# A two-layer trunk on one core: the step into the second layer, and V in natural order

## Chip, cores and metric

The kernel runs on one core of a Trainium2 chip. The metric is the device time of one execution in microseconds; lower is better. Operands and results are 32-bit floats.

## What is computed

The reference is a trunk of two layers over 512 latent tokens and 256 context tokens, each a row of 1024. Every layer has a mixer (two attentions A and B and a gated MLP, fed by one projection `w_in` of the normalised and modulated input) and a mixture of 16 experts in which each expert chooses its tokens: 64 latent and 32 context tokens.

```python
h  = modulate(rmsnorm(x,  g_norm1[i]), sh1,  sc1)
hc = modulate(rmsnorm(xc, g_norm1[i]), sh1c, sc1c)
ka, va, kb, vb, qa, qb, u, v, gates = _split(h @ w_in[i], ...)
...
x = x + gt1 * branch_merge(ya, yb, yc, gates, w_branch[i], w_out[i])
...
x  = x  + gt2  * ec_moe(h2,  w_router[i], w_e1[i], w_e3[i], w_e2[i])
if not last:
    xc = xc + gt2c * ec_moe(h2c, w_router[i], w_e1[i], w_e3[i], w_e2[i])
...
def ec_moe(h, w_r, w1, w3, w2):
    aff = softmax(h @ w_r)
    gate, idx = lax.top_k(swapaxes(aff, 1, 2), cap)
    xin = h[idx]
    hid = silu(xin @ w1) * (xin @ w3)
    ye  = (hid @ w2) * gate
    return zeros.at[idx].add(ye)
```

The last step of a layer, `zeros.at[idx].add(ye)`, is a sum by token index: a token that several experts chose gets the sum of their rows. The output is the latent stream after a final norm.

## The kernel before

**Stages.** A mixer over the context alone (`c0`), one over the latent tokens (`c1`), routing, the experts of layer one (`experts_quad(0)`, L1259), the step into layer two, the mixer of layer two (`c2`, latent tokens, with keys and values of the context), routing, and the experts of layer two (`experts_tiled(1)`), with the final norm. `run()` (L1543) calls them in this order. Instructions of an engine run in the order in which they stand in its queue; a scheduling layer below the program moves them, and the sections on the change show where they stand.

**Weights in two parts.** A product that needs a split weight takes three PE products: high by high, high by low, low by high (`PAIRS`). `split_w` makes the parts: a rounding copy on ACT (L153) and a subtraction on DVE (L155), each 128x1024. They lie in six "w" buffers, so three split chunks fit. The raw chunks come in on SP's queue (`load_w`, L147).

**Experts of layer one.** 96 rows (64 latent, 32 context) are gathered for an expert (L1289, POOL's queue). `mm_set` (L1271) lays the work out in four groups of 32 columns of the array: a 256-wide quarter of the model dimension in each. `stage_1` and `stage_3` make silu and product (L1340), `stage_h` transposes the result (L1321, copies L1325), `stage_2` multiplies by w_e2, scales with the gate (L1347) and adds the rows into the residual in DRAM, in three scatters per expert on POOL's queue (L1349); each scatter waits for the landing of the one before. The loop runs one expert ahead: iteration e makes w_e1 of e+1, then w_e2 of e and w_e3 of e+1. PE's matmul records count two per instruction here.

**The last expert.** Its w_e2 goes another way (`stage_2_rows`, L1353): split weights, 48 products of 128x96 by 512 (L1281), one row scatter, and the rows kept in SBUF. `stage_x` (L1366) loads a table of token numbers (iota, L1369), compares it with the expert's indices to a 96x768 one-hot (L1373), and loads the six residual tiles of 128 tokens from DRAM (L1377), which therefore hold the scatters up to expert 14. `settle(i)` (L1380) adds expert 15's rows to tile i: one-hot by rows on PE (L1386, two halves of 512, two products each), and an add on DVE (L1388).

**The step.** `run()` loads four chunks of the next `w_in` early, settles and normalises tiles 0 to 3 (latent), then 4 and 5 (context), then transposes and modulates (`g_hT`: transposes L301, modulation L307 on ACT, high part L308, low part L309 on DVE) and starts the first keys and queries (`g_qk`, products L327). `norm_tile` (L284) is a square with a sum on ACT (L288), a small scale on DVE (L165), a power on POOL (L167) and a scaling on DVE (L289), in place.

**V.** `g_values` (L368) makes V per chunk of 128 columns in transposed form (weight chunk stationary, tokens moving, L327), copies it to SBUF (L391), transposes it on PE (L380) and copies the 128x128 blocks into V (L382). It runs for both attentions in `c0`, `c1` and `c2`: six passes, 96 transposes.

Memory for tiles is shared by tags; a tile waits until the one that had its buffer is done with. PSUM has four tiles of one bank ("p1") and two of two banks ("p2").

## Time and profile before

| | |
|---|---|
| three runs | 2655.39, 2658.69, 2649.29 us (median 2655.39) |
| the profiled execution | 2656.01 us |
| its span in the profile | 2654.2 us |
| PE busy | 2475.0 us (93%) |
| DVE, ACT, POOL busy | 1318.8, 813.9, 163.4 us |
| bytes moved by DMA | 646.49 MB, mean 244 GB/s |
| mean granted clock of PE | 0.974 |

The profile shows one execution. "Busy" is the time in which an engine ran an instruction; PE's matmul ends are modelled. A row of the timeline gives start, length, engine, line, operation, output and input by the program's names, and the count; in brackets stands the idle time of the engine just before and what ended it. The granted clock is TensorE's, as a share of full speed. SPq and POOLq are the queues in which an engine issues DMAs.

### The profile page before, as it was taken

The numbers are of one execution on the slowest core, as the hardware profiler recorded it, in microseconds if no ns is written. First come the engines' busy times: TensorE is split into PE (matmuls) and PEld (weight loads), VectorE is DVE, ScalarE is ACT, GpSimd is POOL, SyncE is SP. The second block draws the span as 40 slices with busy tenths as digits, with TensorE's granted clock in tenths as the row PEclk, the third lists the DMA queues.
The fourth block names the chain that finished last, engine by engine and source line by source line (L and its number), as shares of the span: only waits on it lengthen the run. The fifth ranks groups of instructions, "written<-read, shape, count | busy, mean of one in ns | idle before, by whom it ended". The sixth has DMA issues, their size and how long they took to land. (4 is left out here: it accounts for less than half of the span.)

```text
span 2654.2 us, 47903 instructions
## 1 busy us (share of the span) xinstructions
PE 2475.0 (93%) x19838; PEld 1709.1 (64%) x19838; DVE 1318.8 (50%) x2608; ACT 813.9 (31%) x1745; POOL 163.4 (6%) x169
## 2 busy tenths in 40 slices
PE   7999999999999979999999699999899969999997
PEld 5888877777778746666666487888788843332222
DVE  7767776878696431111111555656764352332223
ACT  4556455445533300000000445534453220000001
POOL 0000000001000011111111100000000010000000
PEclk9999999999999989999999899999999979999999
DMA  7674664353246779999999553252223569999997
GB/s 277 193 245 151 210 205 133 116 154 102 65 152 229 257 285 379 391 389 383 382 384 395 164 171 120 76 165 74 70 80 125 205 242 413 415 413 414 414 414 292
DMA packets 190954, 646.49 MB, mean 244 GB/s; under 512 B 22352, under 2 KB 32592, under 8 KB 190736
## 3 DMA queue, kind: packets, MB, share of 16 engines
q1 hardware_dynamic: 174352, 608.23, 62.6%
q0 software_dynamic: 10960, 21.50, 3.2%
q10 hardware_dynamic: 5424, 13.70, 1.8%
q8 instruction: 156, 2.56, 0.4%
q14 instruction: 62, 0.51, 0.1%
HBM read 612.94 MB, written 19.92 MB: 238 GB/s over the span
## 5 line engine op out<-in xcount | busy, mean ns | idle before, releaser
L327 PE MATMUL p<-h,w 128*128 128x512 f32 (+1 forms) x4416 | 913.9, 357 | 13.8 <-DVE w L155 5.8
L327 PEld LDWEIGHTS p<-h,w 128*128 128x128 f32 x4416 | 706.3, 190 | 133.9 <-DVE w L155 8.0
L155 DVE TENSOR_TENSOR w<-raw,w 128x1024 fp32r<-128x1024 f32 x224 | 273.5, 1222 | 226.5 <-ACT w L153 223.2
L153 ACT CAST w<-raw 128x1024 fp32r<-128x1024 f32 x224 | 235.1, 1050 | 372.1 <-PE p L327 138.7
L1271 PE MATMUL p<-h,k 128*32 128x256 f32 x3744 | 205.7, 379 | 0.0
L467 PE MATMUL p<-y,w 128*128 128x512 f32 (+1 forms) x864 | 176.6, 361 | 1.1 <-DVE w L155 1.1
L1271 PEld LDWEIGHTS p<-h,k 128*32 128x32 f32 x3744 | 121.2, 110 | 80.1 <-issue 1.2
L264 DVE SCALAR_TENSOR_TENSOR w<-raw,raw 128x1024 bf16<-128x1024 f32 x128 | 155.8, 1221 | 27.6 <-DMA raw<-in_w_adaT 21.4
L467 PEld LDWEIGHTS p<-y,w 128*128 128x128 f32 x864 | 144.3, 191 | 28.0 <-DVE w L155 1.5
L167 POOL TENSOR_TENSOR st<-st,mhalf 128x1 f32<-128x1 f32 x76 | 55.2, 726 | 1619.7 <-DVE st L165 1340.0
L1334 ACT ACTIVATE v<-p 128x768 f32<-128x768 f32 x16 | 13.0, 811 | 458.3 <-PE p L1271 458.3
L1434 PE MATMUL p<-h,k 128*64 128x512 f32 x528 | 128.3, 604 | 8.0 <-DMA h<-in_w_e 7.8
L492 PE MATMUL p<-k,q 128*128 128x256 f32 (+1 forms) x576 | 108.8, 319 | 29.0 <-DMA q<-q 20.0
L1509 DVE TENSOR_TENSOR y<-y,p 128x512 f32<-128x512 f32 x128 | 82.5, 684 | 81.7 <-PE p L1505 81.3
L492 PEld LDWEIGHTS p<-k,q 128*128 128x128 f32 x576 | 84.8, 194 | 44.5 <-issue 11.3
L1349 POOL DMA_INDIRECT x1a<-tg,idx x45 | 69.7, 1549 | 425.3 <-DVE tg L1347 216.1
L1095 PE MATMUL p<-w,h 128*128 128x512 f32 x384 | 91.3, 395 | 1.6 <-DVE w L155 1.1
L1347 DVE SCALAR_TENSOR_TENSOR tg<-p,gate,q 128x256 f32<-128x256 f32 x45 | 19.0, 478 | 142.7 <-PE p L1271 142.7
L1340 DVE TENSOR_TENSOR v<-v,p 128x768 f32<-128x768 f32 x16 | 15.3, 954 | 146.2 <-PE p L1271 137.1
L1434 PEld LDWEIGHTS p<-h,k 128*64 128x64 f32 x528 | 32.9, 136 | 85.3 <-issue 53.4
L1271 PE MATMUL p<-raw,k 128*32 128x256 f32 x1560 | 87.2, 379 | 0.5 <-ACT k L1328 0.5
L1306 DVE TENSOR_TENSOR k<-p,modAlat 128x256 f32<-128x256 f32 x32 | 13.4, 420 | 149.1 <-ACT k L1328 105.0
(339 smaller groups left out, 3128.2 us busy)
## 6 DMA issues: line engine op xcount, KB each, us to landing
h<-in_w_e SPq DMA_DIRECT2D x288, 512.0 KB, 10.7
raw<-in_w_in SPq DMA_DIRECT2D x164, 512.0 KB, 3.8
raw<-in_w_e SPq DMA_DIRECT2D x120, 512.0 KB, 10.1
e<-in_w_e SPq DMA_DIRECT2D x97, 512.0 KB, 10.4
m<-in_w_e SPq DMA_DIRECT2D x94, 512.0 KB, 10.6
raw<-in_w_adaT SPq DMA_DIRECT2D x80, 512.0 KB, 4.5
w<-in_w_e SPq DMA_DIRECT2D x66, 512.0 KB, 10.2
y<-in_w_e SPq DMA_DIRECT2D x52, 512.0 KB, 10.7
```

What stands on the lines that cost most here:

```text
L153: nc.scalar.copy(hi, fr(raw))
L155: nc.vector.tensor_sub(lo, fr(raw), fr(hi))
L167: nc.gpsimd.tensor_tensor(out=r, in0=v, in1=self.mhalf, op=ALU.pow)
L264: nc.vector.scalar_tensor_tensor(out=dump, in0=fr(raw), scalar=1.0, in1=self.cb[v], op0=ALU.mult, op1=ALU.mult, accum_out=self.mod[s, l][: ...
L327: nc.tensor.matmul(ps, lhsT=w[a][:, k * P:(k + 1) * P], rhs=h[k][:, b, :], start=(k == 0 and i == 0), stop=(k == KD - 1 and i == 2))
L467: nc.tensor.matmul(bps, lhsT=wb[a][:, (jj * 4 + k) * P:(jj * 4 + k + 1) * P], rhs=y[k][:, b, :], start=(k == 0 and i == 0), stop=(k == 3 a ...
L492: nc.tensor.matmul(ps, lhsT=Q[:, h, i, qs], rhs=k, start=(i == 0), stop=(i == 1))
L1095: nc.tensor.matmul(banks[i][hf], lhsT=c.mh[k][:, a, i * P:(i + 1) * P], rhs=w[b][:, hf * BW:(hf + 1) * BW], start=(k == 0 and p == 0), sto ...
L1271: nc.tensor.matmul(ps[32 * q:32 * q + 32, r * QW:(r + 1) * QW], lhsT=xT[:, k, 32 * r:32 * r + 32], rhs=w[:, q * QW:(q + 1) * QW], start=(k ...
L1349: nc.gpsimd.indirect_dma_start(out=dst4, out_offset=bass.IndirectOffsetOnAxis(ap=self.idx4[:, r, e:e + 1], axis=0), in_=y[:, r, :], in_off ...
L1434: nc.tensor.matmul(ps[half(h), :], lhsT=xT[:, k, :], rhs=w[:, h * BW:(h + 1) * BW], start=(k == 0), stop=(k == KD - 1))
L1509: nc.vector.tensor_add(xs[i][:, hs], xs[i][:, hs], pss[h])
```

## The change

Six parts, with the names of the new file where they differ:

1. The last expert's w_e2 goes the way of the others, in `last_ctx` (the 32 context rows: 32 products, one column group of 256 wide each per k and quarter) and `last_lat` (the 64 latent rows: 64 products), both over one set of eight raw chunks.
2. Experts 14 and 15 are not scattered. Their scaled rows stay in SBUF as (quarter, row) by 256 columns, and `settle` adds both: for each quarter q the products use the 32 array rows of group q, 8 products for a context tile, 16 for a latent one, each 128x256 into its own PSUM bank. The one-hots are made in `stage_hot`, one expert earlier, from a table loaded ahead of the experts.
3. The residual tiles are loaded right behind the last w_e2 chunks.
4. In `run()`: context half first, settle and normalise the context's tiles, then the latent half, the context's transposes, then for each latent tile settle, store the sum to DRAM by a plain DMA, normalise into another tile; then the latent transposes and `g_qk`.
5. V is made in natural order: tokens stationary, 256 weight columns moving, over two chunks at once; L380 and its copies are gone, and the host lays the chunks of V out in halves.
6. `g_qk` makes the context's keys ahead of the latent ones.

```diff
-    def norm_tile(self, x):
+    def norm_tile(self, x, out=None):
...
-        nc.vector.tensor_scalar_mul(x, x, self.rstd(ss, D))
+        nc.vector.tensor_scalar_mul(x if out is None else out, x, self.rstd(ss, D))
...
-        def place(vt, m, base, g):
-            tp = self.p1([P, m // P, P])
-            for i in range(m // P):
-                nc.tensor.transpose(tp[:, i, :], vt[:, i * P:(i + 1) * P], self.ident)
-            for i in range(m // P):
-                nc.scalar.copy(V[base + i][:, g * P:(g + 1) * P], tp[:, i, :])
-
-        prev = None
-        for g in range(4):
-            w = self.wchunk("w_in", l, c0 + g)
-            for hh, m, base in ((c.h, n, 0),) + (((hc, NCTX, 4),) if hc is not None else ()):
-                ps = self.p1([P, m])
-                yield from self.g_proj(w, hh, m, ps)
...
+        for half in range(2):
+            hs = slice(half * 256, half * 256 + 256)
+            w = [self.wchunk("w_in", l, c0 + 2 * half + i) for i in range(2)]
+            for h, i, o in sets:
+                ps = self.p1([P, 256])
+                for k in range(KD):
+                    for p, (a, b) in enumerate(self.PAIRS):
+                        nc.tensor.matmul(ps, lhsT=h[k][:, a, i * P:(i + 1) * P], rhs=w[k // 4][b][:, (k % 4) * 256:(k % 4 + 1) * 256],
+                                         start=(k == 0 and p == 0), stop=(k == KD - 1 and p == 2))
+                    yield 3 * 256 / 2400
+                nc.scalar.copy(V[o][:, hs], ps)
...
         K = [self.tl([P, 768 if c.lat else NCTX], F32R, "k3") for _ in range(2)]
+        yield from self.g_keys(c, br, idx, wk, K)
         yield from self.g_proj(wk, c.h, n, kps)
...
-        yield from self.g_keys(c, br, idx, wk, K)
...
-        self.gtr = both[:, 1024:]
+        self.row4 = both[:, 512:1280]
+        self.hotc = both[:, 1280:1792].rearrange("p (e c) -> p e c", e=2)
+        nc.scalar.dma_start(self.row4, self.t["iota"].partition_broadcast(P))
...
-            nc.scalar.copy(self.gtr[rows, :], ps[rows, :])
...
-    MFIRST = ["v", "tg"] + MTAGS[:21] + ["tg", "y", "y", "m", "m", "y", "y", "m", "m", "q"]
+    MFIRST = ["v", "tg"] + MTAGS[:21] + ["tg", "y", "y", "m", "m", "y", "y", "m", "m"]
...
-            nc.sync.dma_start(row, self.t["iota"][:n].partition_broadcast(M))
...
+            for j, i in enumerate((4, 5, 0, 1, 2, 3)):
+                xs[i] = self.tl([P, D], F32, self.mtags[(self.mi - len(self.mfirst) + j) % len(self.mtags)])
+                nc.sync.dma_start(xs[i], dst[i * P:(i + 1) * P, :])
...
         def settle(i):
             x = state["xs"][i]
-            for hf in range(2):
-                hs = slice(hf * BW, (hf + 1) * BW)
-                ps = self.p1([P, BW])
-                for j in range(2):
-                    nc.tensor.matmul(ps, lhsT=state["hot"][:, i * P:(i + 1) * P], rhs=state["y"][j][:M, hs],
-                                     start=(j == 0), stop=(j == 1))
-                nc.vector.tensor_add(x[:, hs], x[:, hs], ps)
+            if i % 2:
+                pss = [self.p1([P, QW]) for _ in range(4)]
+            else:
+                two = [self.p2([P, 2, BW]) for _ in range(2)]
+                pss = [two[q // 2][:, q % 2, :QW] for q in range(4)]
+            if i < 4:
+                terms = [(state["hot"][:, j, r, i * P:(i + 1) * P], state["y", LAST + j][:, r, :]) for j in range(2) for r in range(2)]
+            else:
+                terms = [(self.hotc[:, j, (i - 4) * P:(i - 3) * P], state["y", LAST + j][:, 2, :]) for j in range(2)]
+            for n, (a, b) in enumerate(terms):
+                for q in range(4):
+                    rows = slice(32 * q, 32 * q + 32)
+                    nc.tensor.matmul(pss[q], lhsT=a[rows, :], rhs=b[rows, :], start=(n == 0), stop=(n == len(terms) - 1))
+            for q in range(4):
+                if i % 2:
+                    cs = slice(q * QW, (q + 1) * QW)
+                    nc.vector.tensor_add(x[:, cs], x[:, cs], pss[q])
+                elif q % 2:
+                    v = x[:, (q - 1) * QW:(q + 1) * QW].rearrange("p (b c) -> p b c", b=2)
+                    nc.vector.tensor_tensor(out=v, in0=v, in1=two[q // 2][:, :, :QW], op=ALU.add)
             return x
+
+        def last_ctx():
+            e = NEXP - 1
+            state["w"] = list(weights("w_e2", e))
+            ps = self.p1([P, QW])
+            mm_set(ps, state["h", e], state["w"], (2,))
...
+        def last_lat():
...
+            mm_set(ps, state["h", e], state["w"], (0, 1))
...
-        xs = [settle(i) for i in range(4)]
-        for x in xs:
-            self.norm_tile(x)
+        last_ctx()
         xc = [settle(i) for i in (4, 5)]
         for x in xc:
             self.norm_tile(x)
+        last_lat()
+        for _ in self.g_hT(xc, NCTX, self.ab("ctx", 1, 0), c2.hc):
+            pass
+        xs = []
+        for i in range(4):
+            x = settle(i)
+            nc.sync.dma_start(self.x1d[0][i * P:(i + 1) * P, :], x)
+            xs.append(self.tl([P, D], F32, "v"))
+            self.norm_tile(x, xs[i])
         for _ in self.g_hT(xs, NLAT, self.ab("lat", 1, 0), c2.h):
             pass
-        first = interleave(self.g_hT(xc, NCTX, self.ab("ctx", 1, 0), c2.hc), self.g_qk(c2, "a", 0))
+        first = self.g_qk(c2, "a", 0)
```

**Where instructions stand.** In these rows w is a part of a split weight, m, y, e and raw are raw weights or residual tiles, tg scaled rows of an expert, p a PSUM tile, st a column of scales, h the modulated input. First DVE before, at the last w_e2, right behind the transposed product of expert 15:

```order
L1326 TENSOR_TENSOR k_2510_15132<-p_2511_15133,k_2509_15131 128x4x96
L1326 TENSOR_TENSOR k_2510_15132<-p_2512_15139,k_2509_15131 128x4x96
L155 TENSOR_TENSOR w_15166<-m_14754,w_15164 128x1024
L155 TENSOR_TENSOR w_15176<-y_14768,w_15174 128x1024
L1373 TENSOR_SCALAR k_2514_15147<-k_2513_15145,st_15148 96x768
L155 TENSOR_TENSOR w_15186<-y_14782,w_15184 128x1024
L155 TENSOR_TENSOR w_15196<-y_14796,w_15194 128x1024
L155 TENSOR_TENSOR w_15206<-y_14812,w_15204 128x1024
```

The one-hot L1373, made from the iota table k_2513, stands between the splits of w_e2's chunks. DVE in the changed kernel, between the last context normalisation and the context's modulation:

```order
L289 TENSOR_SCALAR raw_15021<-raw_15021,st_15325 128x1024
L155 TENSOR_TENSOR w_15676<-y_15241,w_15674 128x1024
L155 TENSOR_TENSOR w_15744<-y_15243,w_15742 128x1024
L1321 SCALAR_TENSOR_TENSOR tg_15282<-p_2517_15328,gate_114,q_8642 128x256 x2
L155 TENSOR_TENSOR w_15795<-m_15245,w_15793 128x1024
L308 CAST h_15397<-w_2523_15406 128x256
L309 TENSOR_TENSOR h_15397<-w_2524_15410,h_15397 128x256
L309 TENSOR_TENSOR h_15397<-w_2523_15406,h_15397 128x256
L308 CAST h_15398<-w_2526_15419 128x256
```

The splits of w_e2 and the one-hot are gone from there; two splits of chunks of the next `w_in` (y_15241, y_15243) now stand ahead of last_lat's gates L1321, and the modulation (L308, L309) behind them.

Second place, DVE before, in the settlement of the latent tiles:

```order
L1388 TENSOR_TENSOR raw_15155<-raw_15155,p_2550_15278 128x512
L1388 TENSOR_TENSOR raw_15155<-raw_15155,p_2551_15282 128x512
L1388 TENSOR_TENSOR raw_15157<-raw_15157,p_2552_15286 128x512
L1388 TENSOR_TENSOR raw_15157<-raw_15157,p_2553_15290 128x512
L165 TENSOR_SCALAR st_15297<-st_15295 128x1
L1388 TENSOR_TENSOR raw_15159<-raw_15159,p_2570_15326 128x512
L289 TENSOR_SCALAR e_15151<-e_15151,st_15299 128x1024
L165 TENSOR_SCALAR st_15305<-st_15303 128x1
L1388 TENSOR_TENSOR raw_15159<-raw_15159,p_2571_15330 128x512
L289 TENSOR_SCALAR raw_15153<-raw_15153,st_15307 128x1024
```

The adds L1388 of several tiles stand ahead of the first scale L165, and later adds between the scalings L289. DVE in the changed kernel, at the same work:

```order
L1376 TENSOR_TENSOR raw_15023<-raw_15023,p_2534_15453 128x512
L1376 TENSOR_TENSOR raw_15023<-raw_15023,p_2535_15454 128x512
L165 TENSOR_SCALAR st_15478<-st_15476 128x1
L289 TENSOR_SCALAR v_15474<-raw_15023,st_15480 128x1024
L1373 TENSOR_TENSOR raw_15025<-raw_15025,p_2541_15483 128x256
L1373 TENSOR_TENSOR raw_15025<-raw_15025,p_2542_15484 128x256
L1373 TENSOR_TENSOR raw_15025<-raw_15025,p_2543_15485 128x256
L1373 TENSOR_TENSOR raw_15025<-raw_15025,p_2544_15486 128x256
L165 TENSOR_SCALAR st_15512<-st_15510 128x1
L289 TENSOR_SCALAR v_15508<-raw_15025,st_15514 128x1024
L1376 TENSOR_TENSOR raw_15027<-raw_15027,p_2550_15517 128x512
```

A tile's adds (L1376 for even, L1373 for odd tiles) are now followed by its own scale and normalisation, and only then by the adds of the next.

Third place, ACT before, at the first V pass (`c0`), where v_392 is V:

```order
L391 COPY w_86_424<-p_85_399 128x256
L153 CAST w_524<-raw_522 128x1024
L366 DMA q_359<-q_359 64x512
L391 COPY w_93_462<-p_90_432 128x256
L382 COPY v_392<-p_94_464 128x128 x2
L391 COPY w_99_500<-p_98_475 128x256
L382 COPY v_392<-p_100_502 128x128 x2
L153 CAST w_574<-raw_572 128x1024
L576 ACTIVATE e_512,st_515<-p_101_507,st_513 128x256 x2
```

Each chunk is copied transposed (L391), and its blocks are copied into V two at a time (L382). ACT in the changed kernel, at the same pass:

```order
L153 CAST w_464<-raw_462 128x1024
L227 ACTIVATE st_307<-st_303 128x2
L366 DMA q_359<-q_359 64x512
L363 ACTIVATE q_359<-p_77_358 64x256
L390 COPY v_392<-p_88_405 128x256
L153 CAST w_470<-raw_468 128x1024
L366 DMA q_359<-q_359 64x512
L390 COPY v_392<-p_89_431 128x256
L153 CAST w_545<-raw_543 128x1024
```

One copy per token tile and half (L390) is left. w_464 and w_470 are the high parts of the second half's two chunks: the first now stands ahead of V's first copy, the second behind it.

## Rows read from the trace of the kernel before

**Rows 1.** The page's parts 1 and 2: busy us (share) by engine; PE by slice.

```profile
PE 2475.0 (93%) x19838; PEld 1709.1 (64%) x19838; DVE 1318.8 (50%) x2608; ACT 813.9 (31%) x1745; POOL 163.4 (6%) x169
...
PE   7999999999999979999999699999899969999997
```

**Rows 2.** Windows by stage: stretch, length, busy us by engine, granted clock, DMA share, GB/s.

```profile
955.00:1468.00 513.00, 512.51 (x9205) 313.12 (x9197) 78.49 (x193) 25.54 (x47) 81.83 (x60) 1.00 1.03 382
1468.00:1542.00 74.00, 50.37 (x218) 36.20 (x211) 47.79 (x78) 37.14 (x58) 8.59 (x9) 0.82 0.45 143
450.00:650.00 200.00, 190.35 (x1038) 153.36 (x1038) 156.76 (x297) 92.18 (x211) 10.17 (x9) 1.00 0.41 125
2160.00:2640.00 480.00, 442.42 (x1917) 135.19 (x1917) 150.56 (x294) 31.89 (x70) 17.64 (x20) 0.98 0.99 399
1470.00:1475.00 5.00, 3.25 (x20) 2.40 (x19) 3.38 (x4) 4.69 (x6) 0.26 (x1) 1.00 0.28 80
1485.00:1490.00 5.00, 0.00 (x0) 0.00 (x0) 1.42 (x2) 0.00 (x0) 0.00 (x0) 0.50 1.02 332
```

**Rows 3.** SP's waits, then the timeline around the stall: start, length, operation [idle <-releaser].

```profile
SPq L1377 <- DMA x1a<-tg,idx: 15.9, 1, 15.9
...
1444.39 1.54 POOL L1349 DMA_INDIRECT x1a<-tg,idx  x1 [7.19 <-DMA x1a<-tg,idx]
1474.74 1.54 POOL L1349 DMA_INDIRECT x1a<-tg,idx  x1 [5.79 <-DVE w L155]
...
1488.58 0.62 DVE L1373 TENSOR_SCALAR k<-k,st 96x768 fp32r<-96x768 f32 x1 [14.12 <-DMA k<-in_iota]
...
1490.38 2.02 PE L1281 MATMUL p<-w,k 128*96 128x512 f32 x4 [13.89 <-DVE w L155]
```

**Rows 4.** Timeline at the last expert: its w_e3 products, its two copies.

```profile
1464.29 4.07 PE L1271 MATMUL p<-m,k 128*32 128x256 f32 x72
...
1470.13 0.86 ACT L1325 CAST k<-p 128x384 fp32r<-128x384 f32 x2 [22.37 <-PE p L1321]
```

**Rows 5.** Timeline of PE in the second layer's experts: the 64-row products L1505.

```profile
2297.49 0.73 PE L1505 MATMUL p<-tg,k 64*128 64x512 f32 x4
2298.15 1.08 PE L1434 MATMUL p<-raw,k 128*64 128x512 f32 x4
```

**Rows 6.** Split operations from the page, then the normalisation's rows from the timeline.

```profile
L155 DVE TENSOR_TENSOR w<-raw,w 128x1024 fp32r<-128x1024 f32 x224 | 273.5, 1222 | 226.5 <-ACT w L153 223.2
L153 ACT CAST w<-raw 128x1024 fp32r<-128x1024 f32 x224 | 235.1, 1050 | 372.1 <-PE p L327 138.7
...
1508.52 1.06 ACT L288 ACTIVATE w<-raw 128x1024 bf16<-128x1024 f32 x1
...
1509.97 0.69 DVE L1388 TENSOR_TENSOR raw<-raw,p 128x512 f32<-128x512 f32 x1
...
1511.47 0.55 POOL L167 TENSOR_TENSOR st<-st,mhalf 128x1 f32<-128x1 f32 x1 [0.95 <-DVE st L165]
...
1512.95 0.55 POOL L167 TENSOR_TENSOR st<-st,mhalf 128x1 f32<-128x1 f32 x1 [0.93 <-DVE st L165]
...
1520.12 0.75 DVE L289 TENSOR_SCALAR raw<-raw,st 128x1024 f32<-128x1024 f32 x1 [0.44 <-POOL st L167]
...
1527.77 0.42 DVE L309 TENSOR_TENSOR h<-w,h 128x256 fp32r<-128x256 f32 x1
...
1541.25 1.05 ACT L153 CAST w<-raw 128x1024 fp32r<-128x1024 f32 x1 [2.02 <-PE p L327]
```

**Rows 7.** V's transposes by line; then the timeline of PE in the last mixer.

```profile
L380 PE MATMUL p<-ident,w 128*128 128x128 f32 x96 | 16.1, 277 | 4.6 <-ACT w L391 4.6
...
1562.13 0.60 PE L380 MATMUL p<-ident,w 128*128 128x128 f32 x4
1562.48 5.85 PE L327 MATMUL p<-h,w 128*128 128x512 f32 x24
...
1568.30 3.00 PE L327 MATMUL p<-h,w 128*128 128x256 f32 x24
```

More of the change, by code (lines that the diff above doesn't have):

```diff
@@ L404, in g_keys @@
         if not c.lat:
-            for a in range(2):
-                nc.sync.dma_start(self.kd[br][idx, :, a], fr(K[a][:, :NCTX]))
-        elif c.hc is None:
+            return
+        if c.hc is None:
             for a in range(2):
@@ L426, in g_qk @@
         self.split_k(K, slice(0, n), kps)
-        yield from self.g_keys(c, br, idx, wk, K)
+        if not c.lat:
+            for a in range(2):
+                nc.sync.dma_start(self.kd[br][idx, :, a], fr(K[a][:, :NCTX]))
         wq = self.wchunk("w_in", l, c0 + 1 + 2 * idx)
@@ L1215, in gt2 @@
                                     self.ident)
-            rows = (slice(0, 64), slice(64, 96))[i]
-            nc.scalar.copy(self.gtr[rows, :], ps[rows, :])
             for q in range(4):
@@ L1337, in stage_3, with gated @@
             ps = self.p2([P, 3 * QW])
-            mm_set(ps, state.pop(("x", e)), "w_e3", e)
+            mm_set(ps, state.pop(("x", e)), weights("w_e3", e))
             s1 = state["s", e]
             nc.vector.tensor_mul(s1, s1, ps)
+        def gated(y, ps, r, e):
+            nc.vector.scalar_tensor_tensor(out=y[:, r, :], in0=ps, scalar=self.gate4[:, r, e:e + 1],
+                                           in1=self.gtr4[:, r // 2, :], op0=ALU.mult, op1=ALU.mult)
         def stage_2(e):
             ps = self.p2([P, 3 * QW])
-            mm_set(ps, state.pop(("h", e)), "w_e2", e)
@@ L1398, in experts_quad @@
         stage_3(0)
-        for e in range(NEXP):
-            final = e == NEXP - 1
-            if not final:
-                stage_1(e + 1)
-            stage_h(e, final)
-            if final:
-                stage_x()
-                stage_2_rows(e)
-            else:
-                stage_t(e + 2)
-                gather(e + 3)
-                stage_2(e)
-                stage_3(e + 1)
-        return settle
+        for e in range(NEXP - 1):
+            stage_1(e + 1)
+            stage_h(e)
+            stage_t(e + 2)
+            gather(e + 3)
+            if e == LAST - 1:
+                stage_hot()
+            if e == LAST:
+                stage_x()
+            stage_2(e)
+            stage_3(e + 1)
+        stage_h(NEXP - 1)
+        return last_ctx, last_lat, settle
     def moe_raw(self, key):
@@ L1570, in run @@
         self.tail_lat(c1, t["x"])
-        settle = self.experts_quad(0)
+        last_ctx, last_lat, settle = self.experts_quad(0)
         for i, tag in ((4, "y"), (5, "y"), (0, "m"), (1, "m")):
@@ L1610, in blocks, with halves @@
     return w.reshape(k // P, P, n // P, P).transpose(2, 1, 0, 3).reshape(n // P, P, k)
+def halves(w):
+    return w.reshape(2, 4, P, 2, 256).transpose(3, 0, 2, 1, 4).reshape(4, P, 1024)
 def rows2(w):
```

109 lines of the change are left out of this document (42 added, 67 removed).

## Prediction

> **What bounds the kernel now.** Start with the page's busy shares and slices [rows 1]: PE is busy 93% of the span, so what changes PE's work, or lets it idle, changes the time; no other engine is near that. PE reads 9 in most slices, with a 6 at the slice of 1460 to 1526 us, where the change works. The windows by stage [rows 2] say which limit holds where: from 955 to 1468 us (the first layer's experts) PE is busy 512.51 of 513.00 us; from 1468 to 1542 (the step to layer two) only 50.37 of 74.00; in the mixer stages, for which 450 to 650 stands, 190.35 of 200; from 2160 on the DMA share is 0.99 and the second layer's experts wait for weights. Those start with the end of what is before them, so a saving ahead of 2100 us moves the end by as much.
>
> Next the step itself. The queue's waits show one of 15.9 us on SP: the first load of the summed residual waits for the scatters [rows 3]. The timeline shows why: expert 14's third scatter goes out only at 1474.74 us, each of the three waiting for the landing of the one before, and the iota load stands behind those loads on SP's queue. The one-hot made from it (L1373) waits 14.12 us on DVE, where it stands ahead of the split L155 that PE needs, so PE idles 13.89 us ahead of 1490.38 [rows 3].
>
> **The sum: the step.** Anchor: the last w_e3 product ends at 1464.29 + 4.07 = 1468.36 us [rows 4]; nothing ahead of it gets shorter or longer, since PE is full there [rows 2]. (The second "q" buffer goes to `hot`, so one prefetched weight load less; that, the two dropped gtr copies and the early one-hots I cost at nothing, as PE has no gap ahead of 1468 in which a late load would show. Were that cover gone, the load costs what the queue makes up slowly: PE would wait for weights once, some us.)
>
> 1. Gone: the 16 split operations of the last w_e2, its 48 products L1281, the iota load on SP, the scatters of experts 14 and 15, and the 13.89 us idle. SP now passes six x loads right behind the last w_e2 loads; they depend on expert 13's scatters, the last of them issued at 1444.39 [rows 3]. DMA moved only 80 GB/s between 1470 and 1475 [rows 2], so their 3.1 MB finds room (8 us at the 382 GB/s of the experts' stage [rows 2]) and lands by about 1476.
> 2. To 1471.0: product, transposes and two copies as before, 1470.13 + 0.86. Then last_ctx, 64 PE records at 4.07 / 72 = 0.0565 us [rows 4]: 3.6 us, to 1474.6; with its gate, 1475.3.
> 3. The settlements of the context. Four products 256 wide in 32-column groups cost together 8 records, 0.45 us. If 32-row groups also run four side by side, the 8 products of a context tile cost 0.9 us and the 16 of a latent tile 1.8; one after another 3.6 and 7.2. No row shows 32-row groups. The nearest is L1505 with 64-row halves: four such products take 0.66 us to the next instruction (2297.49 to 2298.15) [rows 5], while one of that width costs 0.24 where full-height ones follow each other (24 in 5.85 us [rows 7]), so 0.98 for four in a row. Pairs run together, with some time to enter the shape. I take side by side and keep 7.2 as the other bound. The Trainium skill, "TensorEngine Tiling (Array Packing)", Key Properties, says that a change of tiling mode drains the engine; the 0.66 us, more than two pairs at 0.24 need, agrees with that. By it the six or seven changes of shape in the step would cost some 0.2 us each, an estimate, and the sum would be 1.4 us smaller at most.
> 4. last_lat: 128 records, 7.2 us, to about 1484. The context's normalisation lies beside it. Ahead of last_lat's gates DVE has two L155 on chunks of w_in, loaded into buffers that last_lat's first products release: some 4 us of loading after 1478, then 1.05 and 2 x 1.22 us of splitting [rows 6], so the gates end at about 1486.5. Behind them stand one more L155 and twelve operations of the context's modulation, to about 1492.
> 5. The new limit: DVE's order puts each latent tile's adds and its normalisation L289 ahead of the next tile's adds. Before, adds ran ahead and the tiles followed each other every 1.48 us (POOL's L167 at 1511.47 and 1512.95 [rows 6]). Now each tile pays in series: two adds of 0.69, or four narrow ones of about 0.42 by L309's 256-wide row; the square 1.06; POOL 0.55; L289 0.75 [rows 6]; for the accumulator's read, the small scale L165 and four hops I allow 0.55. That is 4.3 to 4.6 us, 17.6 for four: to about 1509.5. PE's 1.8 us a tile (3.6 at half clock) hides in it. The four plain stores go out on SP, each behind its tile's adds, and the next loads on that queue are of the adaptive weights, which nothing needs for some us.
> 6. From the last normalisation (1520.12 + 0.75) to the end of Q, where ACT's next split is released (1541.25), it took 20.4 us [rows 6], with the modulation of latent and context and four product sets in it. The context's modulation and its K set (3.0 us [rows 7]) now lie ahead, in the tiles' spare time. I take 19.5: Q at 1529, as K's first products still wait for the latent modulation.
>
> Step: 1541.25 - 1529, **12 us gained**. Bounds: 0 (the settlements one after another, rival A), 16 (the gates not held by the splits, some 3.7 us more). The granted clock enters here: between 1485 and 1490, after PE had been idle, it is 0.50 [rows 2], the 1.2 GHz level. The new order leaves PE sparse from 1484 to 1509, so products there may cost double; DVE's 4.4 us a tile hides that, and the latent K set after it may lose 2 us, inside the bounds.
>
> **The sum: V.** 96 transposes L380 go: 16.1 us by busy time, and 4.6 us in which PE waited for L391's copy [rows 7]. From start to the next instruction four take 1562.48 - 1562.13 = 0.35 us, so 96 take 8.4. A set 512 wide becomes two 256 wide: 5.85 against 2 x 3.00 us [rows 7], over 16 sets 0 to 2.4 us, I take 1. ACT gets fewer and shorter copies, beside PE. Against it: a half holds two chunks, four of the six "w" buffers, to its last tile. Only that tile, 3.0 us of PE, covers the splits of the next half's second chunk: 1.05 + 1.22, and with one more 1.22 queued on DVE 3.5 us. I take 0.6 us lost in each of six passes, 4 us with what the order moves. Net 8.4 + 4.6 - 1 - 4 = **8 us**; bounds 0 (the waits take it) and 18 (16.1 + 4.6 - 2.4).
>
> The keys moved ahead in g_qk are the same records. Sum: 20 us. The profiled execution took 2656.01 us for a span of 2654.2; the median of the three runs, 2655.39, is 0.6 below it. 2656 - 20: **forecast 2636 us**, itself 2626 to 2647.
>
> **Rivals.** (A) 32-row groups run one after another. For it: no row shows them. Against: the pairs of L1505. A latent tile then takes PE 7.2 us instead of DVE's 4.4: 4 x 2.8 and 2 x 1.3 on context tiles, 14 us back: 2650. (B) The V halves wait for their second chunk: with two splits queued on DVE 1.05 + 3 x 1.22 = 4.7 us against 3.0, and as much again at the first chunk in three of the passes: 9 x 1.7, 15 us instead of 4, 2647. For it: DVE is busy 156.76 of 200 us in the first latent mixer [rows 2]. Against: other work is woven in there, so that V's products need not follow each other. (C) **Slower**: neither chunk of a half is split ahead. Then each of 12 halves opens with 2 x (1.05 + 1.22) = 4.5 us on an idle PE, 54 us in place of the 4: 2686; it is slower by over 8 us from (20 + 4 + 8) / 12 = 2.7 us a half. Against it: in ACT's order the next half's first chunk stands ahead of V's first copy. (D) Both parts pay in full, the step 16 and V 16: 2624. (E) The stall is not removed: another step of expert 15 takes its place on DVE, and PE still idles 12 us; V alone: 2648.
>
> **Numbers.** Forecast 0.58, A 0.09, B 0.13, C 0.06, D 0.09, E 0.05. Range 2616 to 2650: it takes in A, B, D and E and half of V's upper bound, and leaves out C and the tails. A measurement can tell about 0.3%, 8 us. Faster by more: the forecast, D, most of B and part of A and E, 0.84; same 0.10; slower 0.06.
>
> **What would show it.** PE's idle ahead of 1490 gone; last_ctx and last_lat at 0.0565 us a record; a latent tile's settlement 1.8 us at full clock (A: 7.2); 4.4 us from one latent tile's L289 to the next; the first scores at about 1538 us; small waits ahead of V's products (B, C: 2 us and more each). The prediction is wrong if the end of Q does not move up by 4 us, or if the mixers ahead of 850 us get longer.

## Result and profile after

| | before | after |
|---|---|---|
| median | 2655.39 us (5 runs) | 2631.78 us (5 runs, 2625.77 to 2634.76) |
| the profiled execution, its span | 2656.01, 2654.2 us | 2634.76, 2633.0 us |
| mean granted clock | 0.974 | 0.978 |

The ratio is 0.9915, with an interval of 0.99 to 0.993: 23.6 us faster, where 20 were forecast (2636) and the range was 2616 to 2650.

The page of the changed kernel, busy shares and PE's slices (to be held against [rows 1]):

```profile
PE 2461.0 (93%) x20406; PEld 1718.6 (65%) x20406; DVE 1308.2 (50%) x2609; ACT 788.6 (30%) x1653; POOL 155.2 (6%) x165
...
PE   7999999999899889999999899999999969999997
```

PE is as full as before. The 6 at the slice of the step is now an 8; the other 6, at the routing of the second layer, stands as before. Windows of the changed kernel by stage (columns: the window; its length; busy time of each engine; granted clock; DMA share; GB/s):

```profile
36.00:284.50 248.50, 231.51 (x1904) 223.06 (x1905) 182.09 (x359) 147.34 (x310) 7.98 (x14) 0.98 0.63 204
284.50:854.00 569.50, 542.13 (x3033) 449.06 (x3032) 422.67 (x804) 256.93 (x538) 19.96 (x22) 0.99 0.47 152
...
941.00:1453.30 512.30, 511.80 (x9191) 312.05 (x9179) 78.47 (x193) 25.63 (x47) 80.26 (x59) 1.00 1.03 383
1453.30:1514.60 61.30, 49.17 (x490) 36.79 (x487) 37.57 (x74) 27.39 (x47) 3.31 (x6) 0.94 0.55 204
1514.60:1652.50 137.90, 134.21 (x940) 116.75 (x940) 69.37 (x158) 66.65 (x169) 0.00 (x0) 0.99 0.40 126
1652.50:1795.00 142.50, 140.28 (x891) 119.53 (x890) 85.23 (x157) 56.45 (x125) 1.10 (x2) 0.99 0.34 110
1795.00:1948.70 153.70, 140.03 (x774) 117.01 (x773) 102.69 (x206) 84.90 (x184) 9.16 (x16) 0.97 0.28 81
```

The same stages of the kernel before:

```profile
36.00:292.00 256.00, 234.88 (x1920) 224.97 (x1921) 182.04 (x359) 153.44 (x328) 7.90 (x14) 0.98 0.63 196
292.00:868.00 576.00, 549.20 (x2874) 443.39 (x2874) 424.65 (x806) 260.28 (x560) 20.47 (x22) 0.99 0.48 151
...
955.00:1468.40 513.40, 512.87 (x9205) 313.12 (x9197) 78.49 (x193) 25.54 (x47) 82.23 (x60) 1.00 1.03 381
1468.40:1541.25 72.85, 49.26 (x206) 35.63 (x207) 47.79 (x78) 36.39 (x57) 8.19 (x9) 0.81 0.45 143
1541.25:1680.00 138.75, 136.66 (x871) 113.91 (x870) 72.08 (x163) 70.30 (x189) 0.00 (x0) 1.00 0.44 136
1680.00:1820.00 140.00, 138.25 (x807) 115.23 (x806) 84.68 (x159) 58.32 (x143) 1.10 (x2) 1.00 0.37 115
1820.00:1970.00 150.00, 140.63 (x776) 118.26 (x775) 100.50 (x198) 82.72 (x182) 10.11 (x15) 0.97 0.26 76
```

Read pair by pair:

- The mixer `c0` is 7.5 us shorter (PE busy −3.4, idle −4.1), `c1` 6.5 (busy −7.1), and routing and the experts together 1.1. The last w_e3 product ends at 1453.33 us instead of 1468.36, 15.0 earlier.
- The step is 61.3 us instead of 72.9: 11.6 gained. PE is as busy in it (49.17 against 49.26); what went is idle time, 23.6 to 12.1 us.
- In the mixer `c2` PE's busy time is nearly what it was (414.5 against 415.5 us over its three windows), and PE idles 6.4 us more. By its last gates (L447, at 2089.4 before) the lead has shrunk from 26.6 to 21.3 us, and that lead reaches the end (21.2 by the spans).

So the total is close to the forecast, and its parts are not: 15.0 ahead of the step where V was to give some 4, 11.6 in the step where 12 were forecast, and 5.3 lost in `c2`.

The step in PE's timeline of the changed kernel:

```profile
1447.97 5.36 PE L1269 MATMUL p<-m,k 128*32 128x256 f32 x96
...
1455.89 1.93 PE L1269 MATMUL p<-y,k 128*32 128x256 f32 x32
1457.64 1.91 PE L1269 MATMUL p<-e,k 128*32 128x256 f32 x32
1459.48 2.25 PE L1369 MATMUL p<-tg,q 32*128 32x256 f32 x26
1461.66 3.66 PE L1269 MATMUL p<-y,k 128*32 128x256 f32 x64
1465.14 3.64 PE L1269 MATMUL p<-e,k 128*32 128x256 f32 x64
...
1473.84 2.01 PE L1369 MATMUL p<-tg,q 32*128 32x256 f32 x32 [2.53 <-DVE tg L1321]
...
1500.61 14.20 PE L327 MATMUL p<-h,w 128*128 128x256 f32 x72
1514.65 8.99 PE L387 MATMUL p<-w,h 128*128 128x256 f32 x75
1527.29 2.07 PE L487 MATMUL p<-k,q 128*128 128x256 f32 x8 [3.65 <-DMA q<-q]
```

The two rows of 64 are `last_lat`, 0.057 us a record as predicted. The row at 1473.84 has 32 records, as many as the 16 products of one latent tile give, in 2.01 us. The one wait of 13.89 us [rows 3] is gone. The last row shows a new one: the first scores wait 3.65 us for the queries' DMA.

DVE's rows from the gates to the last normalisation:

```profile
1470.45 2.46 DVE L155 TENSOR_TENSOR w<-y,w 128x1024 fp32r<-128x1024 f32 x2 [1.93 <-ACT w L153]
1472.83 0.87 DVE L1321 SCALAR_TENSOR_TENSOR tg<-p,gate,q 128x256 f32<-128x256 f32 x2
...
1481.88 0.75 DVE L289 TENSOR_SCALAR v<-raw,st 128x1024 f32<-128x1024 f32 x1 [0.73 <-POOL st L167]
...
1485.99 0.75 DVE L289 TENSOR_SCALAR v<-raw,st 128x1024 f32<-128x1024 f32 x1 [0.66 <-POOL st L167]
...
1489.96 0.75 DVE L289 TENSOR_SCALAR v<-raw,st 128x1024 f32<-128x1024 f32 x1 [0.66 <-POOL st L167]
...
1494.12 0.75 DVE L289 TENSOR_SCALAR v<-h,st 128x1024 f32<-128x1024 f32 x1 [0.67 <-POOL st L167]
```

The gates (L1321) stand behind two splits, and the tiles follow each other every 4.08 us ((1494.12 − 1481.88) / 3).

Where the new wait at 1527.29 comes from stands a little later on DVE, with the queue SP beside it:

```profile
1523.22 1.23 DVE L264 SCALAR_TENSOR_TENSOR w<-raw,raw 128x1024 bf16<-128x1024 f32 x1 [3.96 <-DMA raw<-in_w_adaT]
...
1524.49 0.63 DVE L364 SCALAR_TENSOR_TENSOR q<-p,q 64x448 fp32r<-64x448 f32 x1
```

```profile
1517.37 0.33 SPq L147 DMA_DIRECT2D raw<-in_w_adaT  x1
```

L264 reduces a tile of adaptive weights, which nothing needs soon. Its load is issued at 1517.37 only, and in DVE's order it stands ahead of L364, the low part of the second half of the queries. So Q's DMA, and PE with it, waits for a load that has nothing to do with it.

This wait accounts for little of what `c2` lost, though. Over the whole mixer PE waits 12.9 us for Q's DMA, and before it waited 12.0: less at the first scores (0.43), more later. New are two waits for DVE, of transposes inside the two attentions (L590 and L719; columns: what waited for what; us in total, times, longest):

```profile
PE p L719 <- DVE st L748: 2.9, 1, 2.9
PE p L590 <- DVE e L582: 1.9, 1, 1.9
```

PE's busy time, for its part, depends on the granted clock. Here is `c2` from the end of Q to its last gates, before, in the changed kernel, and in a run of the section below that has the changed kernel's program in `c2` (`e7_scatter14`):

```profile
1541.25:2089.40 548.15, 534.94 (x2980) 444.09 (x2979) 320.30 (x601) 246.70 (x559) 12.86 (x20) 0.99 0.35 109
1514.60:2068.10 553.50, 533.60 (x3126) 449.43 (x3126) 319.16 (x599) 243.40 (x523) 12.05 (x20) 0.98 0.33 105
1522.30:2064.80 542.50, 528.44 (x3127) 445.32 (x3126) 318.98 (x599) 243.20 (x523) 12.03 (x20) 1.00 0.34 108
```

The last two differ by 11.0 us: PE is busy 5.2 us less at the higher clock and idles 5.8 less. So the 5.3 us by which `c2` is longer than before are waits and clock, and not more work for PE.

### The profile page after: what moved, and what is told of

Read it like the earlier page. It is cut to its first block, busy times and chain, and to the rows that moved or that the text cites. A ratio compares the mean times of both kernels' runs of the same rounds, so it can differ in the third digit from the quotient of the medians.

```text
span 2633.0 us, 48920 instructions
## 1 busy us (share of the span) xinstructions
PE 2461.0 (93%) x20406; PEld 1718.6 (65%) x20406; DVE 1308.2 (50%) x2609; ACT 788.6 (30%) x1653; POOL 155.2 (6%) x165
## 5 line engine op out<-in xcount | busy, mean ns | idle before, releaser
L327 PE MATMUL p<-h,w 128*128 128x512 f32 (+1 forms) x3648 | 765.8, 359 | 11.0 <-DVE w L155 4.1
L327 PEld LDWEIGHTS p<-h,w 128*128 128x128 f32 x3648 | 585.1, 190 | 112.4 <-issue 7.5
L264 DVE SCALAR_TENSOR_TENSOR w<-raw,raw 128x1024 bf16<-128x1024 f32 x128 | 155.1, 1219 | 31.0 <-DMA raw<-in_w_adaT 30.1
L387 PE MATMUL p<-w,h 128*128 128x256 f32 x1152 | 140.3, 282 | 5.5 <-DVE w L155 5.5
L387 PEld LDWEIGHTS p<-w,h 128*128 128x128 f32 x1152 | 138.2, 191 | 7.1 <-DVE w L155 6.5
L487 PEld LDWEIGHTS p<-k,q 128*128 128x128 f32 x576 | 85.5, 196 | 39.9 <-DMA q<-q 10.4
L1321 DVE SCALAR_TENSOR_TENSOR tg<-p,gate,q 128x256 f32<-128x256 f32 x48 | 20.4, 477 | 147.9 <-PE p L1269 147.9
## 6 DMA issues: line engine op xcount, KB each, us to landing
raw<-in_w_e SPq DMA_DIRECT2D x120, 512.0 KB, 10.1
e<-in_w_e SPq DMA_DIRECT2D x97, 512.0 KB, 10.2
w<-in_w_e SPq DMA_DIRECT2D x66, 512.0 KB, 10.2
```

The lines of the kernel that those rows point to most:

```text
L264: nc.vector.scalar_tensor_tensor(out=dump, in0=fr(raw), scalar=1.0, in1=self.cb[v], op0=ALU.mult, op1=ALU.mult, accum_out=self.mod[s, l][: ...
L327: nc.tensor.matmul(ps, lhsT=w[a][:, k * P:(k + 1) * P], rhs=h[k][:, b, :], start=(k == 0 and i == 0), stop=(k == KD - 1 and i == 2))
L387: nc.tensor.matmul(ps, lhsT=h[k][:, a, i * P:(i + 1) * P], rhs=w[k // 4][b][:, (k % 4) * 256:(k % 4 + 1) * 256], start=(k == 0 and p == 0) ...
L487: nc.tensor.matmul(ps, lhsT=Q[:, h, i, qs], rhs=k, start=(i == 0), stop=(i == 1))
```

## Experiments

The table has one row for each kernel, in the order told below. Columns 4 to 6 are from the profiled execution: how much a stretch is shorter (−) or longer (+) than before's. "Ahead" is up to the first expert's silu (L1334, at 963.9 us before), "step" from there to the end of Q (1541.25 before), "`c2`" from there to its last gates (2089.4 before). The last column is the time in which PE waits for Q's DMA in `c2`, from the waits of a window that holds it. For `e1_v_old`, `e5_gates` and `e8_all` the profiled execution was the fastest of the runs. Each ratio stands against the runs of the kernel before on the same chip.

| kernel | median us (runs) | ratio, interval | ahead | step | `c2` | wait for Q |
|---|---|---|---|---|---|---|
| before | 2655.39 (5) | 1 | 0 | 0 | 0 | 12.0 |
| changed | 2631.78 (5) | 0.9915, 0.99 to 0.993 | −15.0 | −11.6 | +5.3 | 12.9 |
| r_after | 2629.54 (6) | 0.9909, 0.9892 to 0.9926 | −16.6 | −11.7 | +4.0 | 9.9 |
| e1_v_old | 2650.61 (10) | 0.9983, 0.9969 to 0.9998 | −2.5 | −10.2 | +0.3 | 13.3 |
| e1_again | 2650.91 (1) | | +0.3 | −10.1 | +4.0 | 13.7 |
| f1_v_only | 2648.96 (12) | 0.9992, 0.9979 to 1.0005 | −12.8 | −1.9 | +7.7 | 13.7 |
| e2_v_old_c2 | 2627.96 (4) | 0.9893, 0.9872 to 0.9915 | −12.8 | −10.4 | +0.2 | 10.0 |
| e3_plan | 2628.53 (4) | 0.9896, 0.9873 to 0.9918 | −8.3 | −9.8 | −9.8 | 10.5 |
| e4_adds_ahead | 2627.65 (4) | 0.9893, 0.9872 to 0.9914 | −15.5 | −14.3 | +5.3 | 13.4 |
| e5_gates | 2646.85 (12) | 0.998, 0.9968 to 0.9991 | −20.4 | +3.6 | −1.1 | 10.7 |
| e8_all | 2634.14 (6) | 0.994, 0.9922 to 0.9959 | −15.7 | −1.8 | −11.4 | 8.5 |
| e6_keys_back | 2626.4 (6) | 0.99, 0.9882 to 0.9918 | −14.7 | −9.9 | −4.5 | 3.8 |
| e7_scatter14 | 2631.37 (4) | 0.9914, 0.9891 to 0.9937 | −13.8 | −5.1 | −5.7 | 7.4 |
| g_best | 2624.2 (5) | 0.9883, 0.9862 to 0.9904 | −14.2 | −16.0 | −5.8 | 6.1 |

### The step alone, twice: `e1_v_old`, `e1_again`

The changed kernel with V as before (transposed products, L380 and its copies) in all three mixers:

```diff
-        for half in range(2):
-            hs = slice(half * 256, half * 256 + 256)
-            w = [self.wchunk("w_in", l, c0 + 2 * half + i) for i in range(2)]
...
+        for g in range(4):
+            w = self.wchunk("w_in", l, c0 + g)
...
+                if prev is not None:
+                    place(*prev)
```

> V as before in all three mixers (transposed products, L380's 96 transposes, the old chunk layout), the step as in the change. Theory 1 (V accounts for what the trace shows outside the step: 15 us gained ahead of the first experts, 5 us lost in the last mixer; the step gives 11.6): about 12 us under the kernel before, 2643 us, the experts starting within 2 us of 956 us, the last mixer no longer than before. Rival (the 5 us lost in the last mixer come from the new step, for instance from the keys moved ahead): 6 us under, 2649 us, the last mixer still 5 us longer than before.

> V as before with the new step, a second profile. Theory (the profiled run of the first was its fastest by chance; the step's gain is steady, what varies is PE's granted clock and waits in the mixers): the stretch from the last w_e3 product to the first Q again 9 to 12 us shorter than in the kernel before, the difference to the first profile in the mixers. Rival: the step's own length varies by 5 us and more from run to run.

In both profiles the step is 10.1 to 10.2 us shorter, and nothing ahead of it moved by more than 2.5. The runs gained only some 4 us, so the theory's 2643 us was missed; the rival's time came out, but its sign, `c2` 5 us longer, showed in the second profile alone. What stands in the profile of the step is there without the new V. And the two profiles of one kernel differ by 2.8 us ahead of the experts and by 3.7 in `c2`: smaller differences in these two columns say nothing.

### V alone: `f1_v_only`

The kernel before with part 5 of the change and nothing else.

> The kernel before with V in natural order and its chunk layout, nothing else: the old step. Theory 2 (the medians of the runs so far: the step alone is worth 4 us, so V is worth some 19): 2636 us. Theory 1 (the two profiles: V 10 net, the step 12): 2645 us. In the trace the first experts start 10 to 15 us before 956 us, and PE's idle of some 14 us ahead of the last w_e2 is there as before.

12.8 us gained ahead of the experts, where the mixers `c0` and `c1` are, and 7.7 lost in `c2`. By the medians V alone is worth 3 us, and its interval holds no change; both theories (2636 and 2645 us) were missed. The two halves alone, −4 and −3, don't add up to −23.6. Their profiles do only if the faster one of the step is taken: the lead at the second layer's experts is 12.6 and 6.1 us for the two runs of the step alone and 8.2 for V alone, against 21.8 and 24.6 for the two profiles of the change.

### Old V in the last mixer alone: `e2_v_old_c2`

```diff
     def g_values(self, c, br, c0):
+        if c.hc is not None:
+            yield from self.g_values_t(c, br, c0)
+            return
```

> V as before in the last mixer alone. Theory 1 (natural V loses 5 us there): 5 us under the change, 2627 us, PE waits between the last mixer's first Q and 1949 us down by some 4 us. Rival (V gains there too, 2 to 4 us, and the loss has another cause): 2634 to 2636 us.

`c2` no longer loses (+0.2 against +5.3 and +4.0), and the waits of 2.9 and 1.9 us for DVE are gone from it; but the median is within the scatter of the changed kernel's. It says where the 5 us were lost and not that they can be had by this.

### The planner's allowance for transposes: `e3_plan`

`F.plan` spreads side work over a mixer and still allows for the transposes that are gone.

```diff
-        F.plan(4 * (uk + 2 * c.nch * 0.1) + 4 * (u + uk) + 6 * u, 12 * c.nch)
+        F.plan(4 * uk + 4 * (u + uk) + 6 * u, 12 * c.nch)
```

> The two plans of the mixers no longer count time for V's transposes (3.2 us of a latent mixer's estimate each), which natural V does not spend; nothing else. Theory (the estimate is too large, so the woven work runs out before the attention ends, and PE waits there): 2 to 4 us less, PE's waits late in the last mixer (9.2 us for q copies, 2.9 us for a scale) smaller. Rival (the woven work is bound by its own dependences, so where it is spread changes little): within 1.5 us of the change.

`c0` lost all of its 7.5 us (its gates end 0.2 us later than before's) and `c2` gained instead; the time is within the scatter of the changed kernel's. About half of what `c0` lost is clock: its granted clock was 0.967 in this profile and 0.981 in the changed kernel's, which cost some 3.9 us of busy time (an estimate: each busy stretch of the two traces weighted with its clock), and PE idled 2.6 us more. In `c2` the waits for DVE (2.9 and 1.9 us) are gone, which fits the theory that with the old allowance the woven work runs out before the attentions end. They stand in no profile with old V in `c2` or with the new plan; the 2.9 us stand in every one with natural V there and the old plan.

### Adds ahead of the normalisations: `e4_adds_ahead`

```diff
+        sums = [settle(i) for i in range(4)]
...
+            with self.tc.issue_after(state["add"]):
+                self.norm_tile(x, xs[i])
```

> On DVE all four latent tiles' adds stand ahead of the four normalisations, else the change. Theory (DVE's serial order sets 4.08 us a tile): from the first latent add to the end of the last normalisation 10 to 11.5 us instead of 16.4, 5 to 6 us less in all, 2626 us. Rival (PE's settlements, its half clock or the loads of w_in take over as soon as DVE is faster): 0 to 2 us less.

Timeline of its DVE: the tiles follow each other every 1.48 us again, as in [rows 6], once the four adds are through.

```profile
1487.61 0.75 DVE L289 TENSOR_SCALAR v<-raw,st 128x1024 f32<-128x1024 f32 x1 [0.73 <-POOL st L167]
1489.09 0.75 DVE L289 TENSOR_SCALAR v<-raw,st 128x1024 f32<-128x1024 f32 x1 [0.66 <-POOL st L167]
1490.56 0.76 DVE L289 TENSOR_SCALAR v<-raw,st 128x1024 f32<-128x1024 f32 x1 [0.66 <-POOL st L167]
1492.04 0.75 DVE L289 TENSOR_SCALAR v<-h,st 128x1024 f32<-128x1024 f32 x1 [0.66 <-POOL st L167]
```

The step is 2.7 us shorter than the changed kernel's: the series of tiles was the limit there. The medians differ by 1.9 us against `r_after`, which these few runs don't resolve.

### The gates ahead of the splits: `e5_gates`, `e8_all`

`e5_gates` puts the low parts of the early chunks behind the last gates on DVE, and loads the first two of those chunks into other buffers ("m" instead of "y"), so that they come sooner. `e8_all` is that with the edits of `e3_plan` and `e4_adds_ahead`.

```diff
+        with self.tc.issue_after(self.gates):
+            return self.split_w(raw)
...
-        for i, tag in ((4, "y"), (5, "y"), (0, "m"), (1, "m")):
+        for i, tag in ((4, "m"), (5, "m"), (0, "y"), (1, "y")):
```

> The first key and query chunks lie in the buffers that are free earlier (m instead of y), and on DVE no split of an early chunk stands ahead of last_lat's gates. Theory (the gates wait 4 us behind splits whose load lands late): gates done at about 16.5 us behind the end of the last w_e3 product instead of 20.4, 2 to 4 us less, 2628 us. Rival (the context's modulation on ACT and DVE holds the first latent add anyway): 0 to 1 us.

> Plan without the transposes' time, latent adds ahead of the normalisations, gates ahead of the splits with the buffers swapped, all on the change. Theory (the three add, each 3 to 4 us): 9 to 11 us less than the change, 2621 us. Rival (the first two are within the spread of the runs, and the third is covered): 2626 to 2631 us.

`e5_gates` is 15 us slower than the changed kernel by the medians (0.998 of before against 0.9915), where 2 to 4 us less were expected. Its timeline:

```profile
1463.19 1.04 ACT L153 CAST w<-m 128x1024 fp32r<-128x1024 f32 x1 [35.80 <-DMA m<-in_w_in]
1464.14 0.85 ACT L1309 COPY k<-p 128x384 f32<-128x384 f32 x2
...
1464.67 3.64 PE L1272 MATMUL p<-y,k 128*32 128x256 f32 x32 [14.04 <-ACT k L1309]
```

The rounding copy of an early chunk now stands in ACT's order ahead of expert 15's transposed copies. It waits for its load, the copies (ready long before) wait behind it, and PE idles 14.04 us ahead of `last_ctx`. That is the stall of [rows 3] made anew on another engine: there a one-hot that waited for an iota stood ahead of a split, here a split that waits for a weight load stands ahead of a copy. `e8_all` has the same stall (13.66 us), and its 2621 us were missed; its `c2` is the shortest of all, at a granted clock of 1.00.

### Context keys behind the latent ones again: `e6_keys_back`

Part 6 of the change undone.

```diff
         K = [self.tl([P, 768 if c.lat else NCTX], F32R, "k3") for _ in range(2)]
-        yield from self.g_keys(c, br, idx, wk, K)
         yield from self.g_proj(wk, c.h, n, kps)
...
+        yield from self.g_keys(c, br, idx, wk, K)
```

> The change with the context's keys made behind the latent ones, as before. Theory (the context's set of 24 products fills the time in which the latent modulation is not done; behind, it costs its 3 us): 2 to 3 us more than the change, 2634 us, the first Q that much later. Rival (PE is not short of work there): within 1.5 us.

The expectation fell. The step gave back 1.7 us, within what it varies by (9.8 to 11.7 with the change's order), and `c2` is 4.5 us shorter than before's where the changed kernel's is 5.3 longer. The median is 5 us below the changed kernel's (3 below `r_after`), but not of runs beside it: against before on the same chip it is 25.7 us, where the changed kernel had 23.6 and `r_after` 24.9, and the intervals overlap. So the rival, no difference, stands. Waits of PE in `c2`, of this kernel and then of the changed one (columns: what waited for what; us in total, times, longest):

```profile
PE p L485 <- DMA q<-q: 3.8, 6, 1.2
```

```profile
PE p L487 <- DMA q<-q: 12.9, 4, 4.2
```

And DVE's timeline at the first queries of this kernel:

```profile
1521.26 0.63 DVE L364 SCALAR_TENSOR_TENSOR q<-p,q 64x448 fp32r<-64x448 f32 x1 [1.13 <-ACT q L363]
1522.09 1.23 DVE L264 SCALAR_TENSOR_TENSOR w<-raw,raw 128x1024 bf16<-128x1024 f32 x1 [0.20 <-DMA raw<-in_w_adaT]
```

```profile
1526.11 1.21 PE L485 MATMUL p<-k,q 128*128 128x256 f32 x8 [0.48 <-DMA q<-q]
```

In the changed kernel this L264 stands ahead of the second 448-wide L364, here behind it: PE waits 0.48 us for the first scores instead of 3.65 (3.09 in `r_after`). That the key order alone decides it is not shown, though: `f1_v_only` has the same program in `c2` as this kernel and waits 13.7 us. What the table shows over all the kernels with natural V and the old plan is that `c2` is long where that wait is long (7.7 us with 13.7, 5.3 with 12.9 and 13.4, −5.7 with 7.4, −5.8 with 6.1, −4.5 with 3.8), with 4.0 at 9.9 and −1.1 at 10.7 out of line. The granted clock sorts them without exception: 0.985 to 0.988 over `c2` in the four kernels in which it is longer than before's, 0.994 to 0.997 in the four in which it is shorter. The two go together: in the changed kernel the clock is 0.50 in four stretches of `c2` (from 1526.9, 1697.5, 1806.8 and 1892.1 us), each within some 2 us of the end of a wait of PE of 1.9 to 4.2 us; in `e7_scatter14`, `e6_keys_back` and `g_best` there are one or two such stretches.

### Expert 14 scattered as before: `e7_scatter14`

Only expert 15 stays in SBUF; the residual's loads go behind expert 14's scatters.

```diff
-        LAST = NEXP - 2
+        LAST = NEXP - 1
...
-            if e == LAST:
-                stage_x()
...
+        stage_x()
```

> The change, but expert 14 is scattered like the others, only expert 15 is added by one-hots, and the residual loads stand behind expert 14's scatters. Theory (three scatters in a row, some 8 us each, set when the loads start): the loads go out some 13 to 16 us later, PE idles 10 to 14 us ahead of the context's settlement, 2642 us. Rival (last_ctx and last_lat cover the wait, since the settlement of the latent tiles comes late anyway): within 4 us of the change.

Its timeline (the loads were issued at 1449.38 in the changed kernel):

```profile
1465.26 2.26 SPq L1353 DMA_DIRECT2D raw<-x1a  x5
...
1469.23 5.93 PE L1269 MATMUL p<-y,k 128*32 128x256 f32 x64 [5.61 <-DVE raw L1376]
```

The wait for the scatters is there, 5.61 us of PE, and the step is 6.5 us longer than the changed kernel's. PE idles less than the theory's 10 to 14 us. The runs are hardly slower (1.8 us over `r_after` on the same chip, within the intervals), as the rival had it: `c2` gives it back in this profile (−5.7).

### The changed kernel again, and the best combination: `r_after`, `g_best`

`g_best` has the keys back, the adds ahead and the gates ahead of the splits, with the early chunks in the changed kernel's buffers, so that ACT's order stays as it was.

> The changed kernel itself once more, beside the others on the same chip. Theory: 2631 us again (2626 to 2635), so that the two halves, each worth 3 to 5 us alone by their medians, are worth 20 us and more together. Rival (its first runs were on a chip or at a time that favoured it): 2640 us and more.

> The change with the context's keys behind the latent ones again, the latent adds ahead of the normalisations, and the splits of early chunks behind last_lat's gates on DVE, with the early buffers as in the change (so that ACT's cast of an early chunk does not stand ahead of the transposed copies of expert 15). Theory (keys 5 us, adds 4 us, gates 2 to 4 us, all seen singly or in the trace): 2620 us, 9 to 12 us under the change run beside it. Rival (each was within the spread of the runs, or the half clock takes the step's gain back): within 4 us of the change.

`r_after` confirms the result. `g_best` has the shortest step (56.9 us from the last w_e3 product to the end of Q, against 61.3 and 72.9), keeps the gain in `c2`, and is 5.3 us below `r_after` beside it on the same chip, with no run in common, and 30 below the kernel before. That is half of the 9 to 12 us expected. What each of its three edits gives in the runs is not shown.

## Why the prediction came out right, and where not

**The step, forecast 12 us, measured 11.6** (9.8 to 11.7 with the step as the change has it, in six profiles). Its links, in us after the last w_e3 product:

| | forecast | measured |
|---|---|---|
| `last_ctx` done | 6.2 | 6.2 |
| `last_lat` done | 15.6 | 15.5 |
| its gates done | 18.1 | 20.4 |
| last normalisation done | 41.1 | 41.5 |
| end of Q | 60.6 | 61.3 |

The gates came 2.3 us late, because two splits stand ahead of them and ACT waited 2.46 us for the chunk that they split; the tiles made it up with 4.08 us each instead of 4.3 to 4.6. That the two errors cancel is luck. `g_best`, where the gates come first, has them done at 16.4, 4.0 us sooner, so the splits did hold them by about what the upper bound of 16 us allowed (3.7). That its step gains just 16.0 is no proof of that bound, since the adds stand elsewhere too (`e4_adds_ahead` alone: 14.3).

**32-row groups run four side by side.** 2.01 us for a latent tile's 32 records against 1.8 forecast and 7.2 in rival A, which falls. The Trainium skill, "TensorEngine Tiling (Array Packing)", Key Properties, says that different tiles can load weights and multiply in parallel, and that a change of tiling mode drains the engine; the 2.01 us agree with the first, and the 0.2 us over 1.8 would be the size of the second, but no run here measures it by itself.

**Rival E falls**: no single wait idles PE for 12 us in the step; the longest is 5.10 (12.1 in all). But `e5_gates` shows that its mechanism was near: a few rows in another order made it. The time lies between the forecast and rival D (2624), though not for D's reasons: the step didn't pay in full, and `c2` lost a part of what V gave.

**V, forecast 8 us, came near that in this profile (15.0 − 5.3 = 9.7) by the wrong road.** The step of the prediction that failed is "four take 1562.48 − 1562.13 = 0.35 us, so 96 take 8.4", and with it a price per instruction that puts half of the gain into `c2`. What PE's work became shows when its busy time is freed of the clock: each busy stretch counted by the clock granted in it, so that a microsecond at 0.50 counts half (an estimate from the records of each trace, in us; `c0` from 36 us, `c1` and `c0` up to their last gates, `c2` from the end of Q):

| | `c0` | `c1` | `c2` |
|---|---|---|---|
| before | 228.2 | 537.1 | 530.3 |
| step alone, two profiles | 228.4, 227.9 | 537.2, 536.5 | 530.6, 530.7 |
| V alone | 226.0 | 530.2 | 527.4 |
| changed | 225.6 | 530.8 | 526.3 |

So natural V takes 2.6, 6.3 and 4.0 us of work from the mixers, 12.9 in all, where the sum had 8.4 less 1 for the narrower sets: the term was too small, and the place was wrong as well. In `c2` the 4.0 us didn't reach the time: 2.7 went to a lower clock (0.985 against 0.991), and idle time up to the last gates rose by 6.7 (0.9 for Q, 4.8 for L748 and L582, 1 for L709). The prediction had neither the planner, whose old allowance lets these waits arise (`e3_plan`), nor the clock in the mixers. That the sum came out near 8 all the same is luck.

**The waits of the halves, forecast 4 us, are 5.5** (page of the changed kernel, the costliest groups: time busy, mean ns, idle before):

```profile
L387 PE MATMUL p<-w,h 128*128 128x256 f32 x1152 | 140.3, 282 | 5.5 <-DVE w L155 5.5
```

Rivals B (15 us) and C (54 us) fall by this line.

**"The next loads on that queue are of the adaptive weights, which nothing needs for some us"** failed. Nothing needs their result, but the instruction that takes them stands in DVE's order ahead of one that is needed: the first scores wait 3.65 us, where before they waited 0.43. Over `c2` as a whole the waits for Q grew by 0.9 us only, so this is not where most of its 5.3 us went. Whether the moved keys, "the same records", cost time is not shown: with `e6_keys_back` the wait is 0.48 us, but its runs can't be told from the changed kernel's.

**The scatters of expert 14** are worth 6.5 us of the step in the profile, and nothing that the runs resolve.

**Open in part** is why the two halves alone gain so little in timed runs, 4 and 3 us, when together they gain 23.6. For V alone the profile answers it: the work in the three mixers is 12.0 us less, nearly as in the changed kernel, but its mean granted clock is 0.97, and 8.2 us more of PE's busy time than before are lost to the clock (1.9 in the changed kernel). The runs agree: the median clock of V alone is 0.972 where that of before on the same chip is 0.974, that of the step alone 0.974 against 0.973, and that of `r_after` 0.9765 against 0.972. So a part of the 23.6 us is clock that neither half gets alone. Why it is granted when both are there is not shown, and no run isolates it.

## What to carry to other kernels

Look for the wait by walking one engine's queue: an instruction that waits for a load or a landing holds everything behind it, however early its own result is (the iota before, the adaptive weights after, a split's chunk in `e5_gates`). A moved load or an exchanged pair of products is not free because it has the same records; list what stands behind its consumers on their engine. And where side work is woven in by a planner, a term can be right in its sum and wrong in its place, so check it stage by stage. Before two profiles' busy times of PE are compared, look at the granted clock of both: here it hid 2.7 of the 4.0 us that a stage had gained.
